# 576 instead of 640 tokens through the dense expert pass, down projection with v stationary, and one fetched tile's dot products ahead of the dense pass

## The chip, the cores and the metric

The kernel runs on 1 core of one Trainium2 chip. The metric is device microseconds of one execution, the median of several runs. TensorE is called PE, VectorE DVE, ScalarE ACT, GpSimd POOL and the queue that issues most loads SP.

## The reference, cut to what matters

One decoder block over 1024 tokens of width 1024: a mixing sub-layer (gated short convolution and windowed attention, one output projection) and a channel sub-layer that retrieves experts. Only the second is touched:

```python
def peer_ffn(h, wq, keys, u_tab, v_tab):        # 16384 experts of one neuron each
        q = (ht @ wq).reshape(t, PEER_HEADS, 2, PEER_DK)
        sa = jnp.einsum('thd,hnd->thn', q[:, :, 0], keys[0])   # 128 keys on either side
        sb = jnp.einsum('thd,hnd->thn', q[:, :, 1], keys[1])
        ...                                     # top 16 of each, then top 16 of the 256 sums
        eidx = jnp.take_along_axis(cidx, pos, axis=-1)         # 8 heads x 16 experts per token
        g = jax.nn.softmax(top, axis=-1).astype(ht.dtype)
        u = u_tab[eidx]
        v = v_tab[eidx]
        a = jax.nn.gelu(jnp.einsum('thkd,td->thk', u, ht))
        return jnp.einsum('thk,thkd->td', g * a, v)
```

So each token needs 128 rows of u, a dot product with each, and a weighted sum of 128 rows of v. The result is scaled by a gate and added to the residual.

## The kernel before

**Two ways for the experts.** For 640 tokens (0 to 639) the kernel multiplies all 16384 experts by the tokens on PE (the dense pass); a table of gates in DRAM (gd), zero for the experts that a token didn't choose, makes the result right. For the other 384 tokens (three tiles of 128, 640 to 1023) it fetches the chosen rows: POOL issues an indirect DMA for 128 rows of 1024 numbers, one expert for each token of the tile (L713), DVE multiplies u rows by the token's h and sums them (L732, a custom instruction and the read of its accumulator), and later adds v rows times their weight to a sum in PSUM (L740, pq). A tile takes 128 dot products and 128 additions.

**Fronts.** Everything ahead of the dense pass runs in three groups of tokens (0 to 383, 384 to 767, 768 to 1023). A group's front has the input projection, convolution and attention, the output projection (its result is x2T, eight tiles, L464), the queries and scores against the keys, and the search for the top 16 (top16 and select, L555 to L563, ending in eidx, L652). For dense tokens spread() then makes the gate table: for each token two one-hot rows on ACT, POOL or DVE (oi, L675, L676, L678, the engine by the letters of HOT; oj, L683, four tokens on DVE), a matmul (L686, four tokens at a time, here a quad) and a copy to a stage (L687). The search and spread() of one group run inside the next group's front; those of the last group run as the `tail` of dense().

**Dense pass.** 128 columns of 128 experts, four columns to a step, so 32 steps. For a column: uH and uL are made from uraw (two parts of a number, for exact products; uL on POOL, L772), PE makes 48 matmuls of 320 tokens into pa (L788), ACT applies gelu, DVE multiplies by the gates (gw, L807) and makes wdH (ACT) and wdL (DVE, L815). For a step, PE makes 120 matmuls of 512 model columns into pv (L845): 128 tokens of wdH or wdL are the stationary operand, vdH or vdL (vdL on DVE, L832) the moving one. DVE adds each pv to dacc (L864), 128 tokens by 512.

**Background.** gather() is a generator: a call bg() in the code of the front or the dense pass lets it run so many units at a rate (RATE0 for the front, RATE for the dense pass). A unit consumes one row of the ring and fetches the next: six slots of 128 by 1024 numbers. Instructions stand on an engine in the order in which the code issues them, so a unit's place in a queue is where bg() put it.

Of the kernel before, what the change touches and what calls it, by code (L numbers as in the profile page):

```python
# [74 lines left out]
def hymba_peer_kernel(ctx: ExitStack, tc: tile.TileContext, a, out: bass.AP):  # L75
# [34 lines left out]
    x2d = dram.tile([S, D], F32, name="x2d")  # L110
    h2d = dram.tile([GT * P, D], F32, name="h2d")
# [38 lines left out]
    def ada(parts, ap, ring, sums=None):  # L150
        n = 0
        for i in parts:
# [10 lines left out]
            if i < 5:  # L163
                mps = pm.tile([P, 8], F32, name="pm")
                for m in range(NC):
                    PE.matmul(mps[:, m:m + 1], acc[:, P * m:P * (m + 1)], ones[:, 0:1], start=True, stop=True)
                V.tensor_add(mod[:, 8 * i:8 * i + 8], mps, cols[:, COLS["b"][0] + 8 * i:COLS["b"][0] + 8 * i + 8])
            else:
# [138 lines left out]
    def front(t0, T, hs, nxt):  # L307
        nb = T // P
        nd = max(0, min(nb, (DT - t0) // P))
# [793 lines left out]
```

## Time and profile before

| | |
|---|---|
| median of 3 runs | 2874.73 us (2873.96 to 2881.23) |
| span of the profiled execution | 2871.6 us |
| PE busy | 2710.1 us, 94% |
| DVE busy | 2391.0 us, 83% |
| POOL busy | 1727.9 us, 60% |
| ACT busy | 1095.5 us, 38% |
| first gw (L807), where the dense pass begins on DVE | 1076.36 us |
| TensorE clock granted, 1176 to 2866 us | 1.00 |

A share of busy time is an average over the fronts (to about 1076 us) and the dense pass (from there to the end). The two have different limits, so the stages are read apart.

### The profile page before, as it was taken

Reading aid. Unit: us, or ns where it says so; the run is one execution under the profiler, and the core shown is the slowest. Engines: PE = TensorE matmul, PEld = TensorE weight load, DVE = VectorE, ACT = ScalarE, POOL = GpSimd, SP = SyncE. Lnnn points to the kernel's source line nnn. Section 1 sums busy time; section 2 is a strip of 40 time slices with the busy share of each in tenths; the row PEclk is TensorE's granted clock in tenths of the full one; section 3 lists DMA queues with packets and bytes.
Section 4 is the critical chain, followed back from the end, with each engine's and each line's share of the span. In section 5 each row is a group of like instructions: output and inputs, shape, how many; then the busy total and the mean of one; then the engine's idle time right before and its main releaser. Section 6 shows DMA issues by size and latency. Waiting matters only on the chain.

```text
span 2871.6 us, 44952 instructions
## 1 busy us (share of the span) xinstructions
PE 2710.1 (94%) x15567; PEld 2441.8 (85%) x15567; DVE 2391.0 (83%) x4853; ACT 1095.5 (38%) x2193; POOL 1727.9 (60%) x1491
## 2 busy tenths in 40 slices
PE   5999989899888889999999999999999999999998
PEld 3888978788687779889999898999999889989997
DVE  5665899878799778888888898888988888888886
ACT  2455467775476633322222232222223222222221
POOL 3534476665676745666666666666666666656661
PEclk7999989999899989999999999999999999999999
DMA  6647423355334576999999999999999999999995
GB/s 224 230 145 232 123 85 129 139 199 181 99 145 138 203 234 202 347 333 348 331 320 346 348 348 333 348 323 334 337 349 323 324 349 333 331 331 342 331 334 185
DMA packets 345032, 763.69 MB, mean 266 GB/s; under 512 B 31418, under 2 KB 130138, under 8 KB 341860
## 3 DMA queue, kind: packets, MB, share of 16 engines
q0 software_dynamic: 112320, 408.99, 39.2%
q1 hardware_dynamic: 231044, 349.21, 36.4%
q8 instruction: 122, 2.00, 0.3%
q10 hardware_dynamic: 1440, 2.62, 0.2%
q14 instruction: 106, 0.87, 0.1%
HBM read 701.45 MB, written 59.24 MB: 265 GB/s over the span
## 4 chain that ended last, share of the span: by engine, by line
PE 44%; DMA 8%; DVE 6%; issue 4%; POOL 2%; ACT 1%; SPq 0%; DVEq 0%; POOLq 0%; ACTq 0%
PE pv L845 23%; PE pa L788 21%; DMA vraw<-in_v 4%; DMA uraw<-in_uT 2%; DVE pq L740 1%; DVE vdL L832 1%; DVE rows L732 1%; DMA wraw<-in_wq 1%; DVE wdL L815 1%; DVE dacc L864 1%; ACT vdH L831 1%; POOL rows L713 1%; DVE more L732 1%; POOL uL L772 0%; DVE gw L807 0%
## 5 line engine op out<-in xcount | busy, mean ns | idle before, releaser
L788 PE MATMUL pa<-h,uH 128*128 128x320 f32 x4096 | 772.0, 310 | 14.5 <-ACT uH L771 6.3
L788 PEld LDWEIGHTS pa<-h,uH 128*128 128x128 f32 x4096 | 648.2, 189 | 22.0 <-ACT uH L771 7.3
L244 POOL TENSOR_TENSOR wL<-wraw,wH 128x512 fp32r<-128x512 f32 x252 | 360.7, 1440 | 263.2 <-ACT wH L243 224.8
L845 PE MATMUL pv<-vdH,wdH 128*128 128x512 f32 x1275 | 500.2, 392 | 14.7 <-DVE dacc L864 14.5
L845 PE MATMUL pv<-vdL,wdH 128*128 128x512 f32 x1275 | 498.1, 391 | 0.1
L845 PE MATMUL pv<-vdH,wdL 128*128 128x512 f32 x1275 | 497.1, 390 | 0.0
L788 PE MATMUL pa<-h,uL 128*128 128x320 f32 x2048 | 468.9, 310 | 2.9 <-POOL uL L772 2.9
L772 POOL TENSOR_TENSOR uL<-uraw,uH 128x512 fp32r<-128x512 f32 x256 | 343.6, 1343 | 149.5 <-ACT uH L771 140.3
L713 POOL DMA_INDIRECT rows<-in_u,eidx x257 | 259.1, 1008 | 164.7 <-DVE aw L732 100.0
L713 POOL DMA_INDIRECT rows<-in_v,eidx x254 | 252.5, 994 | 160.9 <-DVE pq L740 115.6
L788 PEld LDWEIGHTS pa<-h,uL 128*128 128x128 f32 x2048 | 344.0, 189 | 3.8 <-POOL uL L772 3.8
L740 DVE SCALAR_TENSOR_TENSOR pq<-rows,aw,pq 128x1024 f32<-128x1024 f32 x253 | 324.7, 1284 | 5.0 <-DMA rows<-in_v,eidx 2.5
L864 DVE TENSOR_TENSOR dacc<-dacc,pv 128x512 f32<-128x512 f32 x310 | 212.2, 685 | 137.5 <-PE pv L845 136.7
L831 ACT CAST vdH<-vraw 128x512 fp32r<-128x512 f32 x255 | 152.7, 619 | 437.1 <-DMA vraw<-in_v 386.2
L732 DVE CUSTOM_DVE_ANT_0 rows<-rows,pq 128x1024 f32<-128x1024 f32 x257 | 307.8, 1214 | 10.5 <-DMA rows<-in_u,eidx 10.1
L771 ACT CAST uH<-uraw 128x512 fp32r<-128x512 f32 x256 | 158.4, 620 | 384.1 <-DMA uraw<-in_uT 374.1
L845 PEld LDWEIGHTS pv<-vdH,wdH 128*128 128x128 f32 x1275 | 240.0, 188 | 70.9 <-DVE dacc L864 23.1
L845 PEld LDWEIGHTS pv<-vdH,wdL 128*128 128x128 f32 x1275 | 240.0, 188 | 50.6
L845 PEld LDWEIGHTS pv<-vdL,wdH 128*128 128x128 f32 x1275 | 240.1, 188 | 47.6 <-DVE vdL L832 0.5
L678 POOL TENSOR_SCALAR oi<-iota,tr 128x128 f32<-128x128 f32 x160 | 198.5, 1242 | 109.8 <-PE gps L686 89.4
L832 DVE TENSOR_TENSOR vdL<-vraw,vdH 128x512 fp32r<-128x512 f32 x255 | 193.7, 776 | 74.1 <-ACT vdH L831 73.6
L814 ACT CAST wdH<-gw 128x640 fp32r<-128x640 f32 x128 | 93.1, 728 | 402.6 <-DVE gw L807 393.7
(251 smaller groups left out, 5118.7 us busy)
## 6 DMA issues: line engine op xcount, KB each, us to landing
uraw<-in_uT SPq DMA_DIRECT2D x256, 256.0 KB, 6.3
vraw<-in_v SPq DMA_DIRECT2D x255, 256.0 KB, 6.0
gd<-stage SPq DMA_DIRECT2D x20, 2048.0 KB, 7.5
gt<-gd SPq DMA_DIRECT2D x160, 256.0 KB, 10.2
wraw<-in_w_in SPq DMA_DIRECT2D x108, 256.0 KB, 2.8
wraw<-in_wq SPq DMA_DIRECT2D x96, 256.0 KB, 2.8
wt<-in_w_ada SPq DMA_DIRECT2D x40, 512.0 KB, 4.7
wraw<-in_w_out SPq DMA_DIRECT2D x48, 256.0 KB, 2.7
```

The lines of the kernel that those rows point to most:

```text
L244: G.tensor_tensor(wL, w, wH.bitcast(F32), op=ALU.subtract)
L678: (G if who == "P" else V).tensor_scalar(oi, iota, tr[:, 0, t:t + 1], tr[:, 2, t:t + 1], op0=ALU.is_equal, op1=ALU.mult)
L713: G.indirect_dma_start(out=r, out_offset=None, in_=table, in_offset=bass.IndirectOffsetOnAxis(ap=eidx[:, ti, k:k + 1], axis=0))
L732: V.tensor_tensor_reduce(out=r, in0=r, in1=h2, op0=ALU.mult, op1=ALU.add, scale=1.0, scalar=0.0, accum_out=aw[:, k:k + 1])
L740: V.scalar_tensor_tensor(acc, r, aw[:, k:k + 1], acc, op0=ALU.mult, op1=ALU.add)
L771: A.copy(uH, raw)
L772: G.tensor_tensor(uL, raw, uH.bitcast(F32), op=ALU.subtract)
L788: PE.matmul(AT[j][:, s, 0:n], l[:, c, :], h2[r][4 * h + c][:, s * n:s * n + n], start=(h == 0 and c == 0 and k == 0), stop=(h == 1 and c = ...
L831: A.copy(vH, raw)
L832: V.tensor_tensor(vL, raw, vH.bitcast(F32), op=ALU.subtract)
L845: PE.matmul(pt, l[:, P * tt:P * tt + P], r, start=(m == 0), stop=(m == 3 * J - 1))
L864: V.tensor_tensor(dst, dst, pt, op=ALU.add)
```

## The change

The dense pass takes 576 tokens (128 to 703). The fetched tokens are tokens 0 to 127, a tile of 64 (704 to 767) and two tiles of 128, as GTILES says. A fetch for the tile of 64 has 128 rows as well: two experts for each token, so 448 tokens make 448 fetches of u and 448 of v (384 of each before).

up() now makes one half of the tokens (288) after the other, into pa tiles of one PSUM bank (three in place of two of two banks). The down projection takes v (128 experts by 128 model columns) as the stationary operand and moves 288 tokens of wdH or wdL; so a step has 192 down matmuls of 288 columns, dacc is transposed (model columns on partitions), the last step is one scalar_tensor_tensor with the gate and the residual x2t, and the output of the dense tokens leaves as outT.

The fetched work has two generators. The first, 129 units of GPLAN (the load of h for tile 0 and its 128 dot products), begins in the last group's front with a ring of three slots (ringa has two, ringb one, and holds h in SBUF in place of PSUM), at RATEA 1.75; `drain(gtask[0])` runs what is left of it ahead of dense(). The second has all other units and six slots, in the dense pass. HOT is "APVA" in place of "APVV": one one-hot row in four moves from DVE to ACT.

```diff
-DT0, DT = 0, 640
-G0 = 640
-GT = 3
+DT0, DT = 128, 576
+HN = DT // 2
+GTILES = [(0, 128), (704, 64), (768, 128), (896, 128)]
+GOFF = np.concatenate([[0], np.cumsum([w for _, w in GTILES])]).tolist()
+GT = len(GTILES)
+NG = GOFF[-1]
+OUTS = {"out": (NG, D), "outT": (P, NC, DT)}
 J = 4
 TB = 32
-HOT = "APVV"
-RATE0, RATE = 0.0, 0.49
+HOT = "APVA"
+RATEA, RATE = 1.75, 0.5
...
+GPLAN = []
+for _gi, (_, _w) in enumerate(GTILES):
+    GPLAN += [("h", _gi, 0)] + [("u", _gi, k) for k in range(_w)]
+    GPLAN += [("v", _gi, k) for k in range(_w)] + [("g", _gi, 0), ("x", _gi, 0)]
+NA = 129
...
+        if nxt is None:
+            ra = [t.rearrange("p c t -> p (c t)")[:, 0:D] for t in bigt(ba, "ringa", F32)]
+            rb = gat.tile([P, 2, D], F32, name="ringb", tag="more")
+            gtask.append(add(gather(GPLAN[:NA], ra[0:2] + [rb[:, 0, :]], rb[:, 1, :]), RATEA))
...
+                nc.sync.dma_start(dst[r0:r0 + P - skip, 512 * h:512 * h + 512], xt[skip:P, :])
+
+        dcols, dat = slice(d0 - t0, d1 - t0), slice(d0 - DT0, d1 - DT0)
+        for b, gi in gblocks.items():
+            g0, w = GTILES[gi]
+            to_rows(x2d, GOFF[gi], P - w, b, [x2T], ident)
+        if d1 > d0:
+            for h in range(2):
+                nc.sync.dma_start(x2t[:, 4 * h:4 * h + 4, dat], x2T[h][:, :, dcols])
...
-            for b in (range(nb) if ORDER else [*range(nd, nb), *range(nd)]):
+            for s0, b in blocks:
                 r = yield from select(va[b], iu[b])
-                if b < nd:
-                    yield from spread(t0 // P + b, *r)
-                else:
-                    place((t0 - G0) // P + b, *r)
-                    placed.append(b)
-                    if len(placed) == 1:
-                        gtask.append(add(gather(), RATE0))
+                lo, hi = max(s0, DT0), min(s0 + P, DT0 + DT)
+                if hi > lo:
+                    yield from spread(s0, lo - s0, hi - s0, *r)
+                if b in gblocks:
+                    place(gblocks[b], *r)
+                    placed.append(gblocks[b])
...
+    def gather(plan, slots, held=None):
+
         state = {"n": 0}
-        rows = gat.tile([P, 4, D], F32, name="rows", tag="stage"), gat.tile([P, RING - 4, D], F32, name="more")
 
         def row():
-            n = state["n"] % RING
+            n = state["n"] % len(slots)
             state["n"] += 1
-            return rows[n // 4][:, n % 4, :]
-
-        def fetch(u):
-            ti, n = divmod(u, 2 * P + 2)
+            return slots[n]
+
+        def rows_of(r, src, gi, whole=True):
+            w = GTILES[gi][1]
+            part = src[GOFF[gi]:GOFF[gi] + w, :]
+            G.dma_start(r[P - w:P, :], part)
+            if w < P and whole:
+                G.dma_start(r[0:w, :], part)
+
+        def fetch(unit):
+            kind, gi, k = unit
             r = row()
-            if n == 2 * P:
+            if kind == "h":
+                rows_of(r, h2d, gi)
+            elif kind == "g":
                 G.dma_start(r, g2d)
-            elif n > 2 * P:
-                G.dma_start(r, x2d[G0 + P * ti:G0 + P * ti + P, :])
+            elif kind == "x":
+                rows_of(r, x2d, gi, whole=False)
             else:
-                if n == 0:
-                    state["hr"] = row()
-                    G.dma_start(state["hr"], h2d[P * ti:P * ti + P, :])
-                    state["aw"] = gat.tile([P, P], F32, name="aw", bufs=2)
-                table, k = (a["u"], n) if n < P else (a["v"], n - P)
-                G.indirect_dma_start(out=r, out_offset=None, in_=table,
-                                     in_offset=bass.IndirectOffsetOnAxis(ap=eidx[:, ti, k:k + 1], axis=0))
+                G.indirect_dma_start(out=r, out_offset=None, in_=a[kind],
+                                     in_offset=bass.IndirectOffsetOnAxis(ap=eidx[:, gi, k:k + 1], axis=0))
             return r
 
-        total = GT * (2 * P + 2)
-        ring = [fetch(u) for u in range(RING - 1)]
-        for u in range(total):
-            while (u + RING - 1) // (2 * P + 2) >= len(placed) and len(placed) < GT:
+        ring, at = [], 0
+        for kind, gi, k in plan:
+            while gi not in placed:
                 yield
-            ti, n = divmod(u, 2 * P + 2)
-            if n == 0:
-                aw = state["aw"]
-                h2 = state["hr"]
-                if "pq" in env:
-                    h2 = env["pq"].tile([P, D], F32, name="pq")
-                    A.copy(h2, state["hr"])
+            while at < len(plan) and len(ring) < len(slots) - 1 and plan[at][1] in placed:
+                ring.append(fetch(plan[at]))
+                at += 1
             r = ring.pop(0)
-            k = n % P
-            if n < P:
+            w = GTILES[gi][1]
+            if kind == "h":
+                h2 = held if held is not None else env["pq"].tile([P, D], F32, name="pq")
+                A.copy(h2, r)
+                aws[gi] = gat.tile([P, P], F32, name="aw", bufs=2)
...
-        pa = es.enter_context(tc.tile_pool(name="pa", bufs=2, space=PSUM, side="right", reuse_waits="tile"))
+        pa = es.enter_context(tc.tile_pool(name="pa", bufs=3, space=PSUM, side="right", reuse_waits="tile"))
...
-        def up(*js):
-            for j in js:
-                AT[j] = pa.tile([P, 2, 512], F32, name="pa")
-            for h in range(2):
-                for c in range(4):
-                    for j in js:
-                        uH, uL = U[j][h]
+        def up(j):
+            for s in range(2):
+                AT[j, s] = pa.tile([P, 512], F32, name="pa")
+                for h in range(2):
+                    uH, uL = U[j][h]
+                    for c in range(4):
                         for k, (l, r) in enumerate(((uH, 0), (uH, 1), (uL, 0))):
-                            for s in range(2):
-                                PE.matmul(AT[j][:, s, 0:n], l[:, c, :], h2[r][4 * h + c][:, s * n:s * n + n],
-                                          start=(h == 0 and c == 0 and k == 0), stop=(h == 1 and c == 3 and k == 2))
-            for j in js:
-                U.pop(j)
+                            PE.matmul(AT[j, s][:, 0:n], l[:, c, :], h2[r][4 * h + c][:, s * n:s * n + n],
+                                      start=(h == 0 and c == 0 and k == 0), stop=(h == 1 and c == 3 and k == 2))
+            U.pop(j)
...
-            for tt in range(nt):
-                bg(2.57)
-                next(extra, None)
-                pt = pv.tile([P, 512], F32, name="pv")
-                m = 0
-                for j in js:
-                    vH, vL = VV[j, dh]
-                    for l, r in ((W[j][0], vH), (W[j][0], vL), (W[j][1], vH)):
-                        PE.matmul(pt, l[:, P * tt:P * tt + P], r, start=(m == 0), stop=(m == 3 * J - 1))
-                        m += 1
-                adds.append((g, tt, dh, pt))
-                if len(adds) > LAG:
-                    flush()
+            for x in range(4):
+                for s in range(2):
+                    bg(1.6)
+                    next(extra, None)
+                    pt = pv.tile([P, 512], F32, name="pv")
+                    m = 0
+                    for j in js:
+                        vH, vL = VV[j, dh]
+                        for l, r in ((vH, W[j][0]), (vH, W[j][1]), (vL, W[j][0])):
+                            PE.matmul(pt[:, 0:n], l[:, P * x:P * x + P], r[:, s * n:s * n + n],
+                                      start=(m == 0), stop=(m == 3 * J - 1))
+                            m += 1
+                    adds.append((g, 4 * dh + x, s, pt[:, 0:n]))
+                    if len(adds) > LAG:
+                        flush()
...
-            if g == P // J - 1:
-                r0 = DT0 + P * tt
-                V.tensor_tensor(dst, dst, fin["g2"][dh], op=ALU.mult)
-                V.tensor_tensor(dst, dst, fin["x2"][tt, dh], op=ALU.add)
-                A.dma_start(out[r0:r0 + P, ds], dst)
-
-        fin["x2"], fin["g2"] = {}, {}
+            if g == last:
+                V.scalar_tensor_tensor(dst, dst, mod[:, 40 + dc:41 + dc], fin[dc][:, s * n:s * n + n],
+                                       op0=ALU.mult, op1=ALU.add)
+                A.dma_start(outT[:, dc, s * n:s * n + n], dst)
...
-        for t in gtask:
-            t[1], t[2] = RATE, GC0
+        rows = gat.tile([P, 4, D], F32, name="rows", tag="stage")
+        more = gat.tile([P, 2, D], F32, name="more")
+        slots = [rows[:, x, :] for x in range(4)] + [more[:, x, :] for x in range(2)]
+        add(gather(GPLAN[NA:], slots), RATE, GC0)
...
+    drain(gtask[0])
```

On POOL, at the seam between the last group's front and the dense pass, the kernel before has (wL is a weight of the front's projections, uL one of the dense pass, in_u rows are fetches of the ring):

```order
L244 TENSOR_TENSOR wL<-wraw,wH 128x512 x19
L713 DMA rows<-in_u,eidx 128x1024
L772 TENSOR_TENSOR uL<-uraw,uH 128x512 x2
L713 DMA rows<-in_u,eidx 128x1024
L772 TENSOR_TENSOR uL<-uraw,uH 128x512 x2
L713 DMA rows<-in_u,eidx 128x1024
L772 TENSOR_TENSOR uL<-uraw,uH 128x512 x3
L713 DMA rows<-in_u,eidx 128x1024
L772 TENSOR_TENSOR uL<-uraw,uH 128x512 x2
```

The same place on POOL after the change, the end of a run of fetches into ringa and ringb:

```order
L742 DMA ringa_10023<-in_u,eidx 128x1024
L742 DMA ringb<-in_u,eidx 128x1024
L742 DMA ringa_10022<-in_u,eidx 128x1024
L742 DMA ringa_10023<-in_u,eidx 128x1024
L742 DMA ringb<-in_u,eidx 128x1024
L742 DMA ringa_10022<-in_u,eidx 128x1024
L742 DMA ringa_10023<-in_u,eidx 128x1024
L742 DMA ringb<-in_u,eidx 128x1024
L742 DMA more<-in_v,eidx 128x1024 x2
L802 TENSOR_TENSOR uL<-uraw,uH 128x512 x2
L742 DMA rows<-in_v,eidx 128x1024 x2
L802 TENSOR_TENSOR uL<-uraw,uH 128x512
```

All 128 fetches of the first generator now stand ahead of the first uL of the dense pass, where five fetches stood; the last 50 of them follow each other with few other instructions between.

On DVE, around the first gw of the kernel before (pick, cand, top and pu belong to the search of the last group):

```order
L651 SCALAR_TENSOR_TENSOR pick_12055<-pick_12055,pick_12133 128x128
L559 MATCH_REPLACE cand<-top,cand 128x64
L652 CAST eidx<-pick_12055 128x128
L559 MATCH_REPLACE cand<-top,cand 128x64 x3
L561 MAX top<-cand 128x8 x4
L563 MAX_INDEX pu<-top,cand 128x8 x2
L807 TENSOR_TENSOR gw_11805<-pa,gt_11813 128x640
L807 TENSOR_TENSOR gw_11806<-pa,gt_11813 128x640
L563 MAX_INDEX pu<-top,cand 128x8
L815 TENSOR_TENSOR wdL_11824<-gw_11805,wdH_11798 128x640
L815 TENSOR_TENSOR wdL_11825<-gw_11806,wdH_11799 128x640
```

On DVE ahead of the first gw (L835) after the change, the last three dot products (L760, each with the read of its accumulator) and the first additions of v (L767 and L769):

```order
L760 ISA ringa_10023,aw<-ringa_10023,ringb 128x1024
L760 ISA aw 128x1
L760 ISA ringb,aw<-ringb 128x1024
L760 ISA aw 128x1
L639 SCALAR_TENSOR_TENSOR st_12470<-pf 128x128
L650 TENSOR_TENSOR hot_12489<-hot_12489,idf 128x2048
L766 TENSOR_TENSOR aw<-aw,gate 128x128
L640 TENSOR_TENSOR st<-st,st_12470 128x128
L767 TENSOR_SCALAR pq<-rows,aw 128x1024
L642 TENSOR_TENSOR stb<-pf,st 128x128
L769 SCALAR_TENSOR_TENSOR pq<-rows,aw,pq 128x1024
```

All 128 dot products and 11 additions of v now stand between the sixth x2T tile of the last group and the first gw, and the second search (select) of the last group lies ahead of gw too.

## Rows read from the trace of the kernel before

**Rows 1.** The page's head: span, and busy time of each engine.

```profile
span 2871.6 us, 44952 instructions
PE 2710.1 (94%) x15567; PEld 2441.8 (85%) x15567; DVE 2391.0 (83%) x4853; ACT 1095.5 (38%) x2193; POOL 1727.9 (60%) x1491
```

**Rows 2.** Busy time in stretches: start:end, length, engines, granted clock, DMA share, GB/s.

```profile
390.00:745.00 355.00, 327.96 (x2084) 297.84 (x2084) 297.19 (x987) 242.10 (x576) 223.28 (x176) 0.98 0.43 154
745.00:943.00 198.00, 163.34 (x1101) 140.76 (x1101) 175.86 (x538) 129.66 (x312) 139.36 (x104) 0.90 0.35 123
943.00:1076.00 133.00, 112.67 (x775) 104.82 (x774) 99.48 (x467) 69.28 (x153) 76.45 (x62) 0.90 0.67 228
1076.00:1120.00 44.00, 41.08 (x276) 40.56 (x277) 43.63 (x98) 18.66 (x33) 28.97 (x20) 1.00 0.58 184
1176.00:2866.00 1690.00, 1675.33 (x9348) 1522.20 (x9348) 1465.41 (x1902) 443.57 (x719) 1051.10 (x977) 1.00 0.94 331
1680.00:1760.00 80.00, 79.87 (x439) 71.90 (x438) 68.15 (x110) 19.52 (x32) 55.26 (x51) 1.00 1.01 361
```

**Rows 3.** The chain that ended last: start us, us, what.

```profile
1026.50 1.43 PE pj L247 x12
...
1181.99 7.04 PE pa L788 x48
1189.03 13.62 PE pv L845 x60
```

**Rows 4.** DVE by line, 1400 to 2700 us: count, busy, mean ns, idle before.

```profile
L740 DVE SCALAR_TENSOR_TENSOR pq<-rows,aw,pq 128x1024 f32<-128x1024 f32 x214 | 274.7, 1283 | 2.2
...
L864 DVE TENSOR_TENSOR dacc<-dacc,pv 128x512 f32<-128x512 f32 x233 | 159.5, 685 | 95.2 <-PE pv L845 94.7
...
L815 DVE TENSOR_TENSOR wdL<-gw,wdH 128x640 fp32r<-128x640 f32 x93 | 95.5, 1027 | 3.2 <-ACT wdH L814 3.2
L807 DVE TENSOR_TENSOR gw<-pa,gt 128x640 f32<-128x640 f32 x93 | 76.1, 818 | 2.3 <-ACT pa L805 2.3
```

**Rows 5.** DMA of the dense pass, 1400 to 2700 us.

```profile
DMA packets 201215, 437.26 MB, mean 336 GB/s; under 512 B 17226, under 2 KB 78643, under 8 KB 201117
```

**Rows 6.** DVE in order of time: start us, us, line, operation.

```profile
942.71 0.47 DVE L464 SCALAR_TENSOR_TENSOR x2T<-pj,mod,x 128x256 f32<-128x256 f32 x1
943.10 0.66 DVE L678 TENSOR_SCALAR oi<-iota,tr 128x128 f32<-128x128 f32 x2
943.84 0.69 DVE L683 TENSOR_TENSOR oj<-iota,tr 128x512 f32<-128x512 f32 x1
...
1076.36 1.55 DVE L807 TENSOR_TENSOR gw<-pa,gt 128x640 f32<-128x640 f32 x2 [0.24 <-ACT pa L805]
...
1144.52 1.22 DVE L732 CUSTOM_DVE_ANT_0 more<-more,pq 128x1024 f32<-128x1024 f32 x1
...
1145.66 1.22 DVE L732 CUSTOM_DVE_ANT_0 rows<-rows,pq 128x1024 f32<-128x1024 f32 x1
```

**Rows 7.** The fetches of L713, 940 to 1135 us: landing, and one on POOL's timeline.

```profile
DMA to landing us min/median/max: 4.1/5.4/7.6
...
1133.60 1.05 POOL L713 DMA_INDIRECT rows<-in_u,eidx  x1 [0.30 <-DVE aw L732]
```

**Rows 8.** DVE busy with the dot products (L732) alone, in two stretches of Rows 2.

```profile
943.00:1076.00 133.00, 2.44 (x4) 0.90 0.67 228
1076.00:1120.00 44.00, 9.64 (x16) 1.00 0.58 184
```

**Rows 9.** DVE with gw (L807) alone in the second stretch, then with wdL (L815).

```profile
1076.00:1120.00 44.00, 4.82 (x6) 1.00 0.58 184
1076.00:1120.00 44.00, 7.19 (x6) 1.00 0.58 184
```

**Rows 10.** Matmuls and first activation of one-hot rows of the gate table, 390 to 745 us, by form.

```profile
L686 PE MATMUL gps<-oj,oi 128*128 128x128 f32 x744 | 112.0, 292 | 18.9 <-DVE oi L678 10.9 <-ACT stage L687 2.7 <-POOL oi L678 2.0
...
L675 ACT ACTIVATE oi<-iota,ng 128x128 f32<-128x128 f32 x92 | 36.7, 401 | 25.5 <-PE gps L686 24.6 <-DVE oi L678 0.8
```

More of the change, by code (lines that the diff above doesn't have):

```diff
@@ L74, in hymba_peer_kernel @@
 @with_exitstack
-def hymba_peer_kernel(ctx: ExitStack, tc: tile.TileContext, a, out: bass.AP):
+def hymba_peer_kernel(ctx: ExitStack, tc: tile.TileContext, a, out: bass.AP, outT: bass.AP):
     nc = tc.nc
@@ L108, in colr @@
         return cols[:, COLS[name][0]:COLS[name][1]]
-    x2d = dram.tile([S, D], F32, name="x2d")
-    h2d = dram.tile([GT * P, D], F32, name="h2d")
+    x2d = dram.tile([NG, D], F32, name="x2d")
+    h2d = dram.tile([NG, D], F32, name="h2d")
+    x2t = dram.tile([P, NC, DT], F32, name="x2t")
     g2d = dram.tile([P, D], F32, name="g2d")
@@ L162, in ada @@
                 yield
[L163 to L167, printed above, removed]
-            else:
+            mps = pm.tile([P, 8], F32, name="pm")
+            for m in range(NC):
+                PE.matmul(mps[:, m:m + 1], acc[:, P * m:P * (m + 1)], ones[:, 0:1], start=True, stop=True)
+            V.tensor_add(mod[:, 8 * i:8 * i + 8], mps, cols[:, COLS["b"][0] + 8 * i:COLS["b"][0] + 8 * i + 8])
+            if i == 5:
                 b2 = ap.tile([P, D], F32, name="b2", bufs=1)
@@ L740, in gather @@
                 V.scalar_tensor_tensor(acc, r, aw[:, k:k + 1], acc, op0=ALU.mult, op1=ALU.add)
-            elif n == 2 * P:
+            elif kind == "g":
                 V.tensor_tensor(acc, acc, r, op=ALU.mult)
             else:
-                V.tensor_tensor(r, acc, r, op=ALU.add)
-                G.dma_start(out[G0 + P * ti:G0 + P * ti + P, :], r)
-            if u + RING - 1 < total:
-                ring.append(fetch(u + RING - 1))
+                at_out = out[GOFF[gi]:GOFF[gi] + w, :]
+                V.tensor_tensor(r[P - w:P, :], acc[P - w:P, :], r[P - w:P, :], op=ALU.add)
+                G.dma_start(at_out, r[P - w:P, :])
+                if w < P:
+                    A.copy(r[0:w, :], acc[0:w, :])
+                    G.dma_start(at_out, r[0:w, :], accum_op=ALU.add)
@@ L796, in gload @@
                 GG[g] = gt
-                step = DT // TB // 5
+                step = 3
                 for b in range(0, DT // TB, step):
@@ L855, in flush @@
         def flush():
[L856 to L857 removed]
+            g, dc, s, pt = adds.pop(0)
             if not accs:
[L859 to L860 removed]
+                accs.append(dp.tile([P, NC, DT], F32, name="dacc"))
+            dst = accs[0][:, dc, s * n:s * n + n]
             if g == 0:
@@ L1097 @@
            for k, v in arrays.items()}
-    out = nc.dram_tensor("out", (S, D), F32, kind="ExternalOutput").ap()
+    outs = [nc.dram_tensor(n, w, F32, kind="ExternalOutput").ap() for n, w in OUTS.items()]
     with tile.TileContext(nc) as tc:
-        hymba_peer_kernel(tc, aps, out)
+        hymba_peer_kernel(tc, aps, *outs)
     r = run_bass_kernel_spmd(nc, [{f"in_{k}": v for k, v in arrays.items()}], core_ids=[0])
-    return np.asarray(r.results[0]["out"]).reshape(1, S, D)
+    rows, cols = np.asarray(r.results[0]["out"]), np.asarray(r.results[0]["outT"])
+    y = np.empty((1, S, D), np.float32)
+    for (g0, w), at in zip(GTILES, GOFF):
+        y[0, g0:g0 + w] = rows[at:at + w]
+    y[0, DT0:DT0 + DT] = cols.transpose(2, 1, 0).reshape(DT, D)
+    return y
```

97 lines of the change are left out of this document (46 added, 51 removed).

## The prediction

> **What bounds the kernel now.** The page's head gives the span, 2871.6 us, with PE busy 94% and DVE 83% [rows 1]; that is a mean over stages, so the span was cut into stretches next [rows 2]. In the dense pass (1176 to 2866 us) PE is busy 1675 of 1690 us at the full clock: it is the bound there, DVE stands at 87%, the DMA engines at 94%. In the fronts nothing is full: from 390 to 745 us PE has 92%, from 745 to 943 DVE has 89%, and from 943 to 1076, the last group's search, DVE has 99.5 of 133 us. DVE's timeline gives the two marks that I measure from [rows 6]: the sixth x2T of the last group at 942.7 us and the first gw, with which the dense pass begins, at 1076.4. Behind that mark lie 2871.6 - 1076.4 = 1795.2 us. The chain shows PE's pitch in the dense pass [rows 3]: 48 matmuls of 320 columns in 7.04 us (146.7 ns each), 60 of 512 in 13.62 (227.0 ns); in the front, 12 of 256 took 1.43 (119.2 ns).
>
> **The dense pass: PE saves 135 us.** Before, 128 columns x 48 x 146.7 ns + 3840 x 227.0 ns = 901 + 872 = 1773 us, 55.4 a step. After, 6144 matmuls of up and 6144 of down, all of 288 columns. None of 288 is in the trace; halfway between 256 and 320 is 132.9 ns (the line from 512 through 320 gives 133.3, so the bounds lie close): 12288 x 132.9 = 1633 us, 51.0 a step. At the first gw one column and a half more is done in both. Before, 126 columns are left: 887 + 872 = 1759 of the 1795.2 us, so 36.5 are waits, ramp and end. After: 126.5 columns of 48 x 132.9 ns = 807, down 816, and the same 36.5: **1660 us** from the first gw to the end, 135 less.
>
> **The front: 128 dot products move ahead of the first gw.** The order on POOL puts all 128 fetches ahead of the first uL of the dense pass, that on DVE all 128 dot products, 11 additions of v and the rest of the last select ahead of the first gw. Before, four dots lie ahead of it [rows 8]. All of the moved work stands behind the sixth x2T, so it must fit between the marks. What PE waits for there is gw: its up results fill the three pa tiles, then it stops.
>
> DVE's work between the marks: what stands there now without dots, 99.5 - 2.4 = 97 us [rows 2, 8]. The select that ran after gw: from 1076 to 1120 us DVE is busy 43.6, of which 9.6 are dots, 4.8 gw and 7.2 wdL [rows 8, 9], so 22. Spread has 28 quads left there in place of 16, but with one one-hot row each on DVE in place of two: 28 x (0.69 + 0.33) - 16 x (0.69 + 0.66) = 7 us [rows 6]; 11 when some V rows are slower. The dots: two in a row start 1144.52 and 1145.66, so 1.14 each [rows 6], 128 x 1.14 = 146. Eleven additions x 1.28 = 14 [rows 4]. Sum 286 to 290: **289** is the floor.
>
> The ring of three slots is the other limit. A slot is free after the dot's read; POOL's fetch began 0.3 us after that, and landed 5.4 us later in the median [rows 7]; then the dot, 1.22 + 0.08. That is 7.0 us for three, 2.3 a dot, 128 x 2.3 = 299 us if DVE always came at once. But DVE also does 143 us of other work there, in pieces (a batch of top-16 instructions of some us between dots), and in such a piece the ring stands full and nothing is gained. The two limits are close to each other, so their waits add in part: I take **325** us, between 289 and 345. Of the dots' own length: here both operands are in SBUF (h was in PSUM). Nearest rows: wdL, all from SBUF, 1027 ns, against gw, one from PSUM, 818, for the same 640 columns [rows 4]; at that ratio a dot would be 1.43 and the sum 37 us longer, which the 345 takes in.
>
> The trace shows 4.1 us at least and 5.4 in the median for 524 kB [rows 7]. The Trainium skill, "DMA: Bandwidth & Descriptors", section "Anatomy of one DMA — SWDGE (gpsimd) path", has a fit, 2.0 us plus the bytes over 436 GB/s: an estimate of 3.2 us here, a ring of (0.3 + 3.2 + 1.3) / 3 = 1.6 us a dot, and then only DVE's floor would count. The trace's shortest landing lies above that, so it does not agree.
>
> **Ahead of the mark.** Group 1's front spreads 64 quads in place of 96: PE spent 112.0 us on 744 records, eight to a quad, so 1.2 us a quad, and 32 fewer save 38 us of a stretch in which PE is busy 92% [rows 2, 10]. Against it: each quad has one more one-hot row on ACT, two activations of which the first takes 0.40 us [rows 10], so some 0.8, and in the last group's front (about 50 quads at the pace of 93 in 355 us) that is 40 us more for ACT, 130 to 170 of 198 us, while PE has 163 and DVE 176 [rows 2]. It costs a little where PE waits for one-hot rows. I take **-20**, with -40 to +5 as the bounds.
>
> **Contention in the dense pass.** The bytes don't fall: 768 fetches are left for the dense pass as before, and u and v are loaded whole. Before, 336 GB/s [rows 5] x 55.5 us = 18.7 MB a step. In 51.0 us that wants 366 GB/s; the best 80 us of the trace moved 361 with the DMA engines at 1.01 [rows 2]. At 361 a step takes 51.8 us, at 353 it takes 53.0: 0.8 to 2.0 us x the 29 steps with fetches is 23 to 58. DVE: 1465 / 1690 x 55.5 = 48.1 us a step; after, 16 dacc of 288 columns in place of ten of 512. From 512 to 640 columns a DVE line grows by 1.04 ns a column (685 to 818) [rows 4], so 288 take about 452 ns: 7.2 for 6.9 us, gw 3.6 for 3.3, wdL 0.3 less; 48.4 us of 51.0, 95%. That is near enough to full that PE will sometimes wait for dacc or gw. I take **+25** for both; bounds 0 and 143 (the old mean of 336 GB/s, 55.8 us a step, 4.8 x 30).
>
> **At nothing.** x2t and the transposed output, fewer h2s transfers, one more gate load, eight small matmuls for the gate column, index moves for the tile of 64, one operation less at the last step: all under 5 us, beside PE's work in the fronts or inside the 36.5 us; without that cover they cost their sum, 5 to 10 us. The index moves wait on DVE in SP's queue, and the next wraw loads stand behind them; PE would wait for those for the length of one wait, a few us.
>
> **Sum.** Sixth x2T 943 - 20, + 325 = 1248 for the first gw (1076 before); + 1660 + 25 = 2933 span; by differences 2871.6 - 20 + 191 - 135 + 25 = 2933. The median of the runs lies 3.1 us above the span: **2936 us**.
>
> **Rivals.**
> *Dots for free (faster).* If fetches land in 4.1 us [rows 7] the ring gives 1.9 a dot, 243 us, and DVE is packed at its floor of 289. First gw at 943 - 20 + 289 = 1212, and with 1660 the span is 2872: no change; with the front's 40 it is 1192 and 2852 + 3 = 2855. So it turns at a first gw of 1212: before that the change gains. For it: DVE idles 33 of 133 us between the marks, which dots can fill. Against: the median landing, and the last 50 fetches, which have only the ring.
> *Dense pass bound by bytes or DVE.* At 348 GB/s, between the best and the mean, 18.7 MB take 53.8 us, 2.8 above 51.0, x 30 = 84 in place of 25: 2995. At the old mean the change does not do what it says, the step stays at 55.5: 2936 + 118 = 3054. For it: a DMA share of 0.94 to 1.01 and DVE at 95%. Against: loads are issued ahead, and a loaded queue may reach 361. The Trainium skill, "DMA: Bandwidth & Descriptors", section "Specifications", gives about 358 GB/s as the limit of one core, an estimate of 52.3 us a step, +38 in place of +25; the 80 us at 361 lie on that limit, so the trace agrees nearly.
>
> **Chances.** Forecast, 2885 to 2965 by the bounds of ring, front and contention: 0.54. Dense bound higher: 0.25. Dots for free: 0.21, of which 0.13 faster than 0.3% (what a measurement of this kernel tells from no change) and 0.08 within it. So faster 0.13, same 0.08, slower 0.79. Low 2858 and high 3015 leave about 0.1 out on either side.
>
> **What would show it.** The first gw near 1248, with DVE between the marks at about 89% and idle ends given to the DMA of ringa and ringb; the last fetches 2.3 us apart; PE idle for over 150 us ahead of the dense pass; a 288-column matmul at 133 ns; steps of 51 to 53 us with DVE over 92%. It is wrong if the first gw comes before 1212, if the dots run above 1.3 us, or if steps are over 54 us with a DMA share of 1.0.

## The result, and the profile after

The change makes the kernel slower: 3199.49 us, the median of 4 runs, against 2875.44 before; the ratio is 1.1105, with a 95% interval of 1.1067 to 1.1143. The prediction, 2936 us with 3015 as its upper end, had the direction and was far too low. The profiled execution has a span of 3198.7 us. The page's head:

```profile
span 3198.7 us, 50267 instructions
PE 2698.8 (84%) x17743; PEld 2539.4 (79%) x17743; DVE 2483.6 (78%) x5171; ACT 1155.2 (36%) x2560; POOL 1827.9 (57%) x1609
```

PE is busy about as long as before, 2698.8 against 2710.1 us, in a span that is 327 us longer [rows 1]: the difference is idle time of PE. Where it lies is in the stretches, with the same columns as [rows 2]:

```profile
400.00:560.00 160.00, 140.70 (x797) 123.34 (x797) 98.92 (x299) 125.05 (x330) 79.75 (x64) 0.86 0.24 91
990.00:1100.00 110.00, 69.97 (x385) 61.48 (x385) 88.72 (x213) 53.99 (x132) 77.44 (x66) 0.77 0.78 256
1100.00:1200.00 100.00, 55.85 (x284) 49.32 (x284) 76.79 (x192) 34.39 (x84) 67.23 (x60) 0.67 0.78 255
1200.00:1300.00 100.00, 14.65 (x68) 13.09 (x68) 82.61 (x256) 7.32 (x18) 58.11 (x50) 0.53 0.75 238
1300.00:1378.00 78.00, 20.45 (x72) 16.73 (x72) 56.41 (x133) 5.94 (x14) 34.96 (x31) 0.51 0.90 298
1460.00:3190.00 1730.00, 1600.82 (x11615) 1576.02 (x11615) 1465.06 (x2184) 439.22 (x847) 1056.46 (x992) 0.98 0.93 325
```

Between 1200 and 1378 us PE is busy 35 of 178 us, its clock granted at 0.51 to 0.53 (about the lower level, 1.2 GHz). In the dense pass it is busy 1601 of 1730 us, where before it was 1675 of 1690. DVE's timeline gives the two marks of [rows 6], and the end of the last dot product between them:

```profile
980.26 0.48 DVE L475 SCALAR_TENSOR_TENSOR x2T<-pj,mod,x 128x256 f32<-128x256 f32 x1 [2.66 <-PE pj L256]
...
1334.69 1.23 DVE L760 CUSTOM_DVE_ANT_0 ringb<-ringb 128x1024 f32<-128x1024 f32 x1 [0.27 <-DMA ringb<-in_u,eidx]
...
1378.06 1.19 DVE L835 TENSOR_TENSOR gw<-pa,gt 128x288 f32<-128x288 f32 x3 [15.78 <-DMA gt<-gd]
```

So the sum can be settled term by term against the forecast (span 2933), in us:

| term | forecast | measured | off by |
|---|---|---|---|
| sixth x2T | 923 | 980 | +57 |
| from there to the first gw | 325 | 398 | +73 |
| first gw to the end | 1685 | 1820.6 | +136 |

The three add to 266 us, which is the whole error. The chain that ended last, at the end of the second term (start us, us, what), with pieces left out:

```profile
1318.62 5.27 DMA ringa<-in_u,eidx
1323.92 1.22 DVE ringa L760
...
1325.42 5.15 DMA ringa<-in_u,eidx
1330.59 1.23 DVE ringa L760
...
1335.35 3.96 DMA uraw<-in_uT
...
1341.64 1.28 POOL uL L802
...
1343.32 7.24 DMA h<-h2s
1350.57 18.86 DMA gt<-gd
1369.44 5.75 DMA h<-h2s
```

Fetch and dot alternate up to the last dot; only then come the first loads of the dense pass (uraw, h2s, the gates gt). DVE between the two marks, alone, and what it waited for most there (us in total, times, longest):

```profile
980.26:1378.06 397.80, 313.32 (x803) 0.64 0.79 258
...
DVE ringa L760 <- DMA ringa<-in_u,eidx: 40.1, 39, 4.7
DVE ringb L760 <- DMA ringb<-in_u,eidx: 19.4, 21, 3.5
DVE gw L835 <- DMA gt<-gd: 15.8, 1, 15.8
```

And what PE waited for in the dense pass, before (1176 to 2866 us) and after (1460 to 3190 us):

```profile
PE pv L845 <- DVE dacc L864: 14.2, 13, 4.5
PE pa L788 <- DVE gw L807: 0.5, 1, 0.5
...
PE pa L816 <- DVE gw L835: 71.8, 62, 6.1
PE pv L875 <- DVE dacc L894: 56.8, 28, 4.5
```

### The profile page after: what moved, and what is told of

It reads as the page before. It is cut to its first block, busy times and chain, and to the rows that moved or that the text cites. A ratio compares the mean times of both kernels' runs of the same rounds, so it can differ in the third digit from the quotient of the medians.

```text
span 3198.7 us, 50267 instructions
## 1 busy us (share of the span) xinstructions
PE 2698.8 (84%) x17743; PEld 2539.4 (79%) x17743; DVE 2483.6 (78%) x5171; ACT 1155.2 (36%) x2560; POOL 1827.9 (57%) x1609
## 4 chain that ended last, share of the span: by engine, by line
PE 33%; DVE 26%; DMA 20%; issue 10%; POOL 6%; ACT 4%; SPq 0%; DVEq 0%; POOLq 0%; ACTq 0%
PE pv L875 11%; PE pj L256 9%; DMA vraw<-in_v 6%; PE pa L816 6%; DVE pq L769 5%; DVE rows L760 3%; DVE vdL L861 3%; DMA ringa<-in_u,eidx 3%; POOL wL L253 3%; DMA rows<-in_u,eidx 2%; PE gps L711 2%; DVE dacc L894 2%; DMA ringb<-in_u,eidx 2%; DVE more L760 1%; DMA more<-in_v,eidx 1%
## 5 line engine op out<-in xcount | busy, mean ns | idle before, releaser
L816 PE MATMUL pa<-h,uH 128*128 128x288 f32 x4096 | 848.2, 302 | 204.2 <-ACT uH L801 116.7
L875 PE MATMUL pv<-wdH,vdH 128*128 128x288 f32 x2040 | 612.5, 300 | 56.8 <-DVE dacc L894 56.8
L816 PE MATMUL pa<-h,uL 128*128 128x288 f32 x2048 | 613.5, 300 | 2.8 <-POOL uL L802 2.8
L875 PE MATMUL pv<-wdH,vdL 128*128 128x288 f32 x2040 | 610.8, 299 | 0.4 <-DVE vdL L861 0.4
L875 PE MATMUL pv<-wdL,vdH 128*128 128x288 f32 x2040 | 609.4, 299 | 0.0
L802 POOL TENSOR_TENSOR uL<-uraw,uH 128x512 fp32r<-128x512 f32 x256 | 341.2, 1334 | 209.5 <-ACT uH L801 202.9
L875 PEld LDWEIGHTS pv<-wdH,vdH 128*128 128x128 f32 x2040 | 391.7, 192 | 63.7 <-DVE dacc L894 63.7
L875 PEld LDWEIGHTS pv<-wdH,vdL 128*128 128x128 f32 x2040 | 391.1, 192 | 0.8 <-DVE vdL L861 0.8
L875 PEld LDWEIGHTS pv<-wdL,vdH 128*128 128x128 f32 x2040 | 391.5, 192 | 0.1
L769 DVE SCALAR_TENSOR_TENSOR pq<-rows,aw,pq 128x1024 f32<-128x1024 f32 x296 | 379.4, 1282 | 5.4 <-DMA rows<-in_v,eidx 3.3
L894 DVE TENSOR_TENSOR dacc<-dacc,pv 128x288 f32<-128x288 f32 x496 | 221.1, 450 | 117.3 <-PE pv L875 116.7
L760 DVE CUSTOM_DVE_ANT_0 rows<-rows,pq 128x1024 f32<-128x1024 f32 x212 | 255.3, 1212 | 19.9 <-DMA rows<-in_u,eidx 19.6
L711 PE MATMUL gps<-oj,oi 128*128 128x128 f32 x1152 | 204.6, 316 | 61.1 <-POOL oi L703 20.9
```

What stands on the lines that cost most here:

```text
L711: PE.matmul(ps[:, x, :], ois[x], oj[:, x, :], start=True, stop=True)
L760: V.tensor_tensor_reduce(out=r, in0=r, in1=h2, op0=ALU.mult, op1=ALU.add, scale=1.0, scalar=0.0, accum_out=aws[gi][:, k:k + 1])
L769: V.scalar_tensor_tensor(acc, r, aw[:, k:k + 1], acc, op0=ALU.mult, op1=ALU.add)
L802: G.tensor_tensor(uL, raw, uH.bitcast(F32), op=ALU.subtract)
L816: PE.matmul(AT[j, s][:, 0:n], l[:, c, :], h2[r][4 * h + c][:, s * n:s * n + n], start=(h == 0 and c == 0 and k == 0), stop=(h == 1 and c = ...
L875: PE.matmul(pt[:, 0:n], l[:, P * x:P * x + P], r[:, s * n:s * n + n], start=(m == 0), stop=(m == 3 * J - 1))
```

## The experiments

Two theories stood against each other for each term. Each run below is a single execution with a profile, except e12, which was timed four times. The four timed executions of the changed kernel lie 24 us apart (3179.74 to 3203.27), so a difference between two single spans that is not larger than that shows nothing. "Seam" is the time from the sixth x2T to the first gw, "dense" from the first gw to the end of the span; all times are in us.

| run | sixth x2T | first gw | seam | dense | span |
|---|---|---|---|---|---|
| before | 943 | 1076 | 134 | 1795 | 2871.6 |
| after | 980 | 1378 | 398 | 1821 | 3198.7 |
| e1 no front dots | 977 | 1137 | 160 | 1949 | 3086.5 |
| e2 no dense fetches | 977 | 1357 | 381 | 1636 | 2993.5 |
| e3 APVV | 916 | 1334 | 418 | 1818 | 3151.6 |
| e4 PSUM 4 + 2 | 976 | 1374 | 399 | 1847 | 3221.4 |
| e5 fetches only | 974 | 1374 | 400 | 1705 | 3079.0 |
| e6 DVE work only | 979 | 1355 | 375 | 1740 | 3094.7 |
| e7 half the front dots | 980 | 1224 | 244 | 1827 | 3050.2 |
| e8 no front dots, APVV | 911 | 1061 | 150 | 1941 | 3001.9 |
| e9 tile of 64 left out | 978 | 1367 | 389 | 1720 | 3087.6 |
| e10 before, APVA | 1019 | 1158 | 139 | 1803 | 2961.1 |
| e11 PSUM 4 + 4, pq in SBUF | 979 | 1374 | 395 | 1903 | 3277.3 |
| e12 e8 and e11 | 912 | 1064 | 152 | 2066 | 3130.1 |

### The seam: e1 and e7

```diff
-RATEA, RATE = 1.75, 0.5
+RATEA, RATE = 1.75, 0.57
...
-NA = 129
+NA = 0
...
```

> The first generator is empty: all fetched work runs in the dense pass, at a rate of 0.57 units in place of 0.5 so that it still ends with it. If the 128 dots and their three-slot ring hold up the seam, the first gw falls from 1378 us to 1115 +- 20 (the sixth x2T at 980 plus the 134 us of the kernel before). If the seam is long for another reason (slow clock, fewer slots of PSUM), the first gw stays above 1250. The dense pass takes 130 dots more: between 1820 us (they fill DVE's idle time) and 1980 (they add at 1.25 us each), so 2935 to 3095 in total.

The first gw comes at 1137 us: the dots and their ring hold up the seam. 128 of them cost 398 - 160 = 238 us. The dense pass took 129 us more. In it lie 136 more dots and additions, and about 33 us of the last search and gate table on DVE that the changed kernel does ahead of its first gw; so 129 us is not the price of the units alone.

```diff
-            gtask.append(add(gather(GPLAN[:NA], ra[0:2] + [rb[:, 0, :]], rb[:, 1, :]), RATEA))
+            gtask.append(add(gather(GPLAN[:65], ra[0:2] + [rb[:, 0, :]], rb[:, 1, :]), RATEA))
...
```

> The first generator does 64 of the 128 dot products, the other 64 are left out of the whole kernel. If the ring of three slots sets the seam, the first gw falls by 64 x 2.6 = 165 us, to about 1213; if DVE's own work does, by 64 x 1.2 = 77, to about 1300. The 44 us from the last dot to the first gw stay if they are the start of the dense pass behind the ring.

The first gw falls by 154 us, 2.4 us for each of the 64 dots. That is the pace of the last 64 dots: in the changed kernel the 64th starts at 1183.1 us (1180.4 in e7) and the 128th at 1334.7. It is nearer to the ring's forecast than to a dot's own length, but DVE is busy 125 us of that stretch of 153, so the run does not separate the ring from DVE. The first 64 dots, which run beside the front, cost 244 - 160 = 84 us.

The last dot of e7 starts at 1180.4 and the first gw at 1223.6, so 42 us lie behind the dots, as was expected. But the start of the dense pass stood behind something else there. SP's queue has the last weights of the front (wraw) and then the first load of the dense pass (h2s, the tokens), in the kernel before, in the changed kernel, in e7 and in e1 (a line's second number reaches from the first to the last of its loads):

```profile
1030.49 4.95 SPq L240 DMA_DIRECT2D wraw<-in_wq  x4
1035.49 0.42 SPq L909 DMA_DIRECT2D h<-h2s  x1
...
1172.74 40.00 SPq L249 DMA_DIRECT2D wraw<-in_wq  x4
1334.49 0.33 SPq L931 DMA_DIRECT2D h<-h2s  x1
...
1168.01 17.78 SPq L249 DMA_DIRECT2D wraw<-in_wq  x4
1185.89 0.38 SPq L933 DMA_DIRECT2D h<-h2s  x1
...
1090.52 9.14 SPq L249 DMA_DIRECT2D wraw<-in_wq  x4
1099.71 0.54 SPq L931 DMA_DIRECT2D h<-h2s  x1
```

From that load to the first gw it is 41, 44, 38 and 37 us: the start of the dense pass takes about as long in all of them. Of these four, only the changed kernel's load waited for a dot (SP's waits, 1000 to 1378 us):

```profile
SPq L931 <- DVE aw L760: 121.7, 1, 121.7
```

It waited for the last dot's read. The ring's ringa and the tiles of dense() are taken from the same memory, one after the other, so the dense pass could load nothing before the ring was done. The 238 us of e1 are these: with the dots beside it the front's last weights come 113 us later (1212.7 against 1099.7, where the sixth x2T is 3 us later), the load then waits 122 us, and the start takes 6 us longer.

### The fronts: e3 and e10

```diff
-HOT = "APVA"
+HOT = "APVV"
```

> HOT is APVV as in the kernel before, all else as changed. If the extra one-hot row on ACT stretched the fronts, the sixth x2T comes near 945 us in place of 980 and the total falls by about 30 us. If the fronts are longer because 32 fewer quads leave PE idle and its clock low, the x2T stays after 965 and the total moves by less than 15 us.

The sixth x2T moves by 64 us, to 916. The stretch from 400 to 560 us, in the kernel before and in this run (the changed kernel's stands in the result):

```profile
400.00:560.00 160.00, 147.91 (x949) 131.37 (x948) 142.41 (x415) 121.94 (x304) 105.64 (x82) 0.96 0.36 135
...
400.00:560.00 160.00, 142.83 (x906) 123.91 (x907) 142.49 (x386) 115.53 (x288) 107.09 (x79) 0.94 0.29 109
```

906 matmuls in place of 797, at a clock of 0.94 in place of 0.86, and DVE takes 142 us where it had 99. Between 243 and 605 us PE waits 13 us for ACT, where it waited 26. The total fell by 47 us: the seam is 418 us long and takes 20 of the 64 back, with 20 us more of DVE's time between the marks (334 against 313).

In the kernel before, the same letter the other way:

```diff
-HOT = "APVV"
+HOT = "APVA"
```

> The kernel before with one change, HOT from APVV to APVA. If one-hot rows on ACT slow the fronts by themselves, its sixth x2T moves from 943 us to about 1010 (64 us were seen with 64 quads in the front of the second group, here 93), with a granted clock of about 0.86 between 400 and 560 us, and the total rises by 50 to 80 us. If they only hurt where quads are few, it moves by less than 20 us.

```profile
400.00:560.00 160.00, 139.79 (x854) 120.63 (x853) 108.05 (x302) 135.55 (x358) 86.53 (x70) 0.93 0.33 121
...
1019.11 0.48 DVE L464 SCALAR_TENSOR_TENSOR x2T<-pj,mod,x 128x256 f32<-128x256 f32 x1 [2.66 <-PE pj L247]
```

The x2T comes 76 us later and the span is 89.5 us longer, more than the 50 to 80 expected: the letter alone slows the fronts, in either kernel. The clock I expected was wrong: 0.93, not 0.86. ACT is busy 136 of 160 us, and between 243 and 605 us PE waits 26 us for ACT in place of 10. How much of the 64 and 76 us is waiting for ACT and how much is the lower clock, no run separates.

### The dense pass: e2, e5, e6, e4 and e9

```diff
-        add(gather(GPLAN[NA:], slots), RATE, GC0)
```

> The second generator is left out, so the rows of the fetched tokens are not written; the front and the seam stay (first gw at 1378 us). If the dense pass loses its time to the fetched work (DVE's queue and the bytes), it falls from 1820 us to 1660 or less and PE's waits for gw and dacc from 129 us to under 30. If it loses it to too few PSUM tiles between PE, ACT and DVE, PE still waits more than 80 us for gw and dacc and the stage stays above 1740.

1636 us, and PE waits for nothing between 1460 and 2900 us:

```profile
1460.00:2900.00 1440.00, 1440.00 (x10870) 1440.00 (x10869) 568.09 (x1016) 400.51 (x789) 304.70 (x227) 1.00 0.34 107
```

PE's own part was forecast rightly: 1440 us for 10870 matmuls is 132.5 ns each (133 forecast). The whole difference, 1821 - 1636 = 185 us, goes with the fetched work. Its two halves apart, first the fetches with short DVE work (32 of 1024 numbers), then DVE's work on rows that are never fetched:

```diff
+                m = D if held is not None else 32
-                V.tensor_tensor_reduce(out=r, in0=r, in1=h2, op0=ALU.mult, op1=ALU.add, scale=1.0,
+                V.tensor_tensor_reduce(out=r[:, 0:m], in0=r[:, 0:m], in1=h2[:, 0:m], op0=ALU.mult, op1=ALU.add, scale=1.0,
...
-                V.scalar_tensor_tensor(acc, r, aw[:, k:k + 1], acc, op0=ALU.mult, op1=ALU.add)
+                V.scalar_tensor_tensor(acc[:, 0:32], r[:, 0:32], aw[:, k:k + 1], acc[:, 0:32], op0=ALU.mult, op1=ALU.add)
```

> In the dense pass the dot products and the additions of v work on 32 of 1024 numbers; all fetches stay. DVE there loses some 800 us of busy time. If the bytes hold the dense pass (18.7 MB a step at 330 to 361 GB/s), it stays at 1760 us or more in place of 1820. If DVE's queue holds it, PE waits nearly nothing and the stage falls to 1640 to 1690.

```diff
+            if held is None:
+                return r
...
+        for r in slots:
+            V.memset(r, 0.0)
         add(gather(GPLAN[NA:], slots), RATE, GC0)
```

> The other half: in the dense pass nothing is fetched (rows are zero and stay), all dot products and additions of v stay at full length. If DVE's queue holds the dense pass, it stays at 1760 us or more; if the bytes do, it falls to 1640 to 1690. If only both together hold it, this run and the one before both fall below 1720.

The dense pass of the fetches-only run, with PE's longest wait:

```profile
1460.00:3060.00 1600.00, 1549.97 (x11518) 1540.66 (x11517) 765.36 (x2164) 439.87 (x844) 1064.74 (x990) 0.99 0.97 350
...
PE pv L876 <- DVE dacc L895: 40.8, 26, 4.4
```

and of the run with DVE's work only, with PE's one wait (1460 to 3000 us):

```profile
1460.00:3080.00 1620.00, 1546.00 (x11448) 1527.58 (x11447) 1469.48 (x2152) 425.45 (x839) 351.53 (x239) 0.99 0.33 101
...
PE pa L818 <- DVE gw L837: 66.3, 66, 3.2
```

Neither theory holds alone: both runs lie between the two forecasts. The fetches cost 1705 - 1636 = 68 us, at a DMA share of 0.97 and 350 GB/s; DVE's work costs 1740 - 1636 = 104, with DVE at 91% and no fetch at all. Together that is 172 of the 185, as near as single runs can tell. The fetches, too, reach PE through DVE's queue: in e5 DVE is busy 48% only, but it waits 311 us for fetched rows, and PE waits for the dacc behind them. With DVE's work alone PE waits 66 times, one us on average; a dot or an addition that stands ahead of gw in DVE's queue takes 1.2 to 1.3 us. POOL issues no fetches in e6 either, so what its issuing costs is not shown apart.

```diff
-        pa = es.enter_context(tc.tile_pool(name="pa", bufs=3, space=PSUM, side="right", reuse_waits="tile"))
+        pa = es.enter_context(tc.tile_pool(name="pa", bufs=4, space=PSUM, side="right", reuse_waits="tile"))
...
-        pv = es.enter_context(tc.tile_pool(name="pv", bufs=3, space=PSUM))
+        pv = es.enter_context(tc.tile_pool(name="pv", bufs=2, space=PSUM))
```

> Four PSUM tiles for up and two for down in place of three and three. If PE's wait for gw (72 us) comes from running out of pa tiles, it falls below 30 us, the wait for dacc rises by less than that, and the dense pass is 25 to 60 us shorter. If DVE is late for both whatever the banks, the waits only change places and the dense pass moves by less than 15 us.

The wait for gw is gone, the one for dacc rose from 57 to 131 us (70 times), and the stage is 26 us longer. The waits change places, as the second theory had it, but that theory had the stage within 15 us. The gain of 25 to 60 us that the first theory had did not come; that two tiles for down are worse than three, 26 us in one run hardly show.

```diff
-        add(gather(GPLAN[NA:], slots), RATE, GC0)
+        add(gather([u for u in GPLAN[NA:] if u[1] != 1], slots), RATE * 0.83, GC0)
```

> The tile of 64 tokens is left out of the dense pass (its 128 fetches and 131 units less; the rate is lowered in proportion, so that the rest is spread over the whole stage). If fetched work costs the same per unit from the first on (184 us for 770 units, 0.24 each), the dense pass falls from 1820 us to about 1790. If the first units are hidden and the last ones pay in full (129 more cost 129 us in the first run), it falls to about 1690 to 1700.

```profile
1460.00:3060.00 1600.00, 1538.81 (x11421) 1521.75 (x11419) 1298.28 (x1954) 431.73 (x835) 933.93 (x855) 1.00 0.89 305
...
PE pv L875 <- DVE dacc L894: 32.7, 22, 2.5
PE pa L816 <- DVE gw L835: 27.6, 37, 2.2
```

The dense pass falls by 100 us for 131 units, 0.77 each; nearer to the second theory. Some 640 units cost 84 us, the next 131 cost 100, and e1's further units, with the search beside them, 129. In these runs fetched work grows dearer the more of it there is.

One thing in this run does not fit a price that comes from full engines alone. DVE is busy 81% here and the DMA share is 0.89, both less than in the kernel before (87%, 0.94), and yet PE waits 60 us where it waited 15. What else differs is the new form of the pass: a tile of up is 24 matmuls, 3.2 us of PE at 132.5 ns, where it was 48 in 7.04 us [rows 3], and there are three of them in place of two. Whether the smaller tiles make PE feel a late DVE sooner is a rival that no run here tests.

### Put together: e8, e11 and e12

e8 has the edits of e1 and e3.

> No dots in the front and HOT as before. If the two losses add, the first gw comes at 1137 - 62 = 1075 and the total at 3088 - 62 = 3026; the dense pass then loses its 1950 us alone. If the slow front had covered something else, the total falls by less than 40.

The span is 85 us shorter than that of e1, where 62 was expected: the two losses add, and more. Its first gw, 1061 us, is earlier than the 1076 of the kernel before, yet it ends 130 us later, all of it in the dense pass, where PE waits 189 us for gw and dacc (1200 to 2960 us).

```diff
-        env["pq"] = es.enter_context(tc.tile_pool(name="pq", bufs=1, space=PSUM, side="right", reuse_waits="tile"))
+        env["pq"] = es.enter_context(tc.tile_pool(name="pq", bufs=1))
```

and pa and pv with four tiles each:

> The sum pq of the fetched tokens lies in SBUF in the dense pass, so PSUM has four tiles for up and four for down in place of three and three. If PE's 129 us of waits for gw and dacc come from DVE being late by a few dots at a time, which more tiles absorb, they fall below 60 us and the dense pass from 1820 us to 1700 to 1770. If DVE and the transfers are short of time as such, the waits stay above 100 us and the stage within 20 us of 1820.

The dense pass got longer, 1903 us, and for a reason neither theory had. DVE and POOL by line from 1460 to 3190 us (columns as in [rows 4]), first of this run:

```profile
L769 DVE SCALAR_TENSOR_TENSOR pq<-rows,aw,pq 128x1024 f32<-128x1024 f32 x271 | 403.2, 1488 | 19.0 <-DMA rows<-in_v,eidx 17.0
L760 DVE CUSTOM_DVE_ANT_0 rows<-rows,pq 128x1024 f32<-128x1024 f32 x212 | 302.1, 1434 | 23.6 <-DMA rows<-in_u,eidx 23.4
...
L742 POOL DMA_INDIRECT rows<-in_v,eidx x274 | 388.3, 1417 | 106.9 <-issue 48.6 <-DVE pq L769 42.5 <-DVE dacc L894 6.4
```

and of the changed kernel:

```profile
L769 DVE SCALAR_TENSOR_TENSOR pq<-rows,aw,pq 128x1024 f32<-128x1024 f32 x279 | 357.6, 1282 | 5.2 <-DMA rows<-in_v,eidx 3.3
L760 DVE CUSTOM_DVE_ANT_0 rows<-rows,pq 128x1024 f32<-128x1024 f32 x212 | 255.3, 1212 | 19.9 <-DMA rows<-in_u,eidx 19.6
...
L742 POOL DMA_INDIRECT rows<-in_v,eidx x280 | 277.4, 991 | 167.1 <-DVE pq L769 120.3 <-issue 27.4 <-DVE gw L835 3.0
```

With pq in SBUF a dot takes 1434 ns in place of 1212, an addition 1488 in place of 1282, and the issue of a fetch on POOL 1417 in place of 991. In e4, where the tiles changed but pq stayed in PSUM, a dot took 1213 ns, so it is pq's place and not the tiles. What more tiles would give without that stays open.

> No dots in the front, HOT APVV, and pq in SBUF with four and four tiles of PSUM. First gw at 1061 us as in the run with the first two edits. The dense pass, 1941 us there, falls by what the tiles give in the run beside this one, 50 to 120 us, so 2880 to 2950 in total, if the tiles absorb DVE's lateness; it stays at 3000 if DVE is short of time.

3131 us, ratio 1.0884 to before (1.0846 to 1.0923), and a dense pass 126 us longer than e8's. The dots on the tile rows take 1380 ns where e8's take 1213, their fetches 1381 where e8's take 976: the same as in e11. No version here beats the kernel before.

## Why the prediction was wrong, step by step

- **PE's saving in the dense pass: right.** 1636 us alone, against the forecast's 1660 without contention.
- **The step "I take +25 for both" failed most.** It measured +185 over PE alone (136 of the error; PE's own part came out 24 below). Its two causes were named with their bounds, 0 and 143, and the value was taken near the low end, as if PE's 51 us of work a step could lie over a DVE at 95% and 366 GB/s at once. The forecast 53.0 us a step at 353 GB/s was good (53.3 in e5, at 350). What was left out is that DVE's work costs 104 us on its own, and that the two losses come to about their sum. In the kernel before DVE had 7 us a step to spare (87%), and PE waited 15 us in all for it. e9 says that a fuller DVE is not all of it; how much the smaller tiles add stays open. The rival "dense pass bound by bytes or DVE" was the case, and its price, 84, was too low as well.
- **The Trainium skill's limit** ("DMA: Bandwidth & Descriptors", "Specifications") is about 358 GB/s for one core. e5's 350 GB/s at a DMA share of 0.97 agrees nearly, and e5 lost 68 us, where the estimate from that limit was 38.
- **The step "I take 325 us" for the ring failed next.** It was 289 us of DVE's work and 36 of waiting; it measured 313 and 85, above the upper bound of 345. DVE's idle 33 us there were put down as room "which dots can fill", and that was right: in the kernel before DVE waited 24 us for scores from ACT and 9 for one-hot matmuls, and 2 and 5 us of that are left. What was sized too low is the waiting for the ring's fetches, 60 us. What was missed is the start of the dense pass, some 40 us in every run with its fetches. In the kernel before SP begins it beside the search; the ring moved it behind the last dot through shared memory. DVE filled 26 of those 42 us with the additions and the rest of the search, so that 16 of waiting for the gates are left. The order on POOL had shown uL behind all fetches; what the loads on SP wait for was not asked.
- **The dots' length.** The forecast 1.14 us is the distance of two starts; a dot itself took 1.22. In the ring the median stayed at 1.22 and the mean of the 128 rose to 1.39, because 17 of them took 1.4 us or more, up to 3.5. That is some 22 us, the larger part of DVE's 24 above its 289. So the ratio of wdL to gw was no measure of it: operands in SBUF did not make every dot longer.
- **Ahead of the mark, "-20": the sign was wrong.** With APVV the sixth x2T came 27 us earlier than before, where 38 were forecast for the fewer quads. But the letter in HOT cost 64 us; I had priced it as "a little". ACT was read as not full (170 of 198 us), and that was the mistake: at 78 to 85% busy its queue already delays what PE waits for (26 us in place of 13 between 243 and 605 us), and the granted clock is lower with it (0.86 against 0.94 between 400 and 560 us). The shares of the two are not separated.

## What to carry to other kernels

PE time that is saved in a stage is a gain only as far as the next engine can follow. Before a stage with DVE at 87% is made shorter, price it with each of its other loads alone, fetches and DVE's work; here they cost 68 and 104 us, and together 185. Work that is moved ahead of a stage must be followed to the memory that it holds: here the stage's first load waited 122 us for the last read of that memory. An engine at about 80%, with a queue of short instructions that the critical engine waits for, is not free to take more: one letter cost 64 us here.

## What was not expected of the hardware

A DVE instruction with both operands in SBUF can take twice its time while POOL works. Two dots of the ring (both operands in SBUF) and the POOL instructions that were running when they began, in the changed kernel:

```profile
1005.77 1.28 POOL L253 TENSOR_TENSOR wL<-wraw,wH 128x512 fp32r<-128x512 f32 x1
1005.81 2.33 DVE L760 CUSTOM_DVE_ANT_0 ringa<-ringa,ringb 128x1024 f32<-128x1024 f32 x1 [1.27 <-DMA ringa<-in_u,eidx]
...
1012.25 1.26 POOL L253 TENSOR_TENSOR wL<-wraw,wH 128x512 fp32r<-128x512 f32 x1
1012.34 2.26 DVE L760 CUSTOM_DVE_ANT_0 ringa<-ringa,ringb 128x1024 f32<-128x1024 f32 x1 [1.42 <-DMA ringa<-in_u,eidx]
```

Each ends 1.09 us after POOL's instruction, nearly a dot's own length, as if it had begun only then. All 17 long dots of the ring began while POOL was running, 12 of them behind wL. With pq in PSUM none of the 320 dots of the dense pass took over 1.23 us; with pq in SBUF (e11) 68 of 320 took over 1.4, all begun while POOL was running, and the median stayed at 1.22. POOL suffers too, even its issue of fetches (991 to 1417 ns in e11). The Trainium skill has this: "GPSIMD Engine Reference", section "1. Specifications", says that GpSimd's SBUF interfaces are shared with VectorE and that they collide with DVE instructions that have two SBUF inputs. The run agrees, with about 0.4 us a fetch and 0.2 us a dot on average here.
